# Embedding lookup plus positions: stores of two sequences, 16 KB for each partition, in place of one, 8 KB

## The chip, the cores and the metric

One core of one Trainium2 chip. The metric is the device time of one execution in microseconds (us), as the profiler gives it; the span of the profile is the same execution without about 1.7 us of launch.

A few words used below. GpSimd (POOL) issues the gathers: one gather is an indirect DMA that fetches 128 rows of the table, 2 KB each, 262 KB together. VectorE (DVE) adds, ScalarE (ACT) copies, SyncE (SP) issues loads and stores. The profile counts the packets of all DMA queues against the same 16 DMA engines. A "row" of a chunk is one 128 x 512 float32 piece, the product of one gather.

## The reference

```python
batch, seq_len, vocab_size, d_model = 32, 512, 50000, 512
def reference(indices, embedding_table, position_embed):
    token_embed = embedding_table[indices]
    return (token_embed + position_embed).astype(np.float32)
```

33.6 MB are gathered from random rows and 33.6 MB are written. Positions are 1 MB, indices 0.13 MB.

## The kernel before

A chunk is one sequence: partition p holds positions 4p to 4p+3, so K = 4 gathers fill it, and a whole store has 8 KB contiguous for each partition. The positions are copied once to PSUM, and VectorE adds them in place. The first and last sequences are stored in smaller pieces.

```python
P = 128; K = 4; SLOTS = 24; LANES = 16
HALVES = (2, 2); QUARTERS = (1, 1, 1, 1)
...
for b in range(B):
    if b <= 1 or b == B - 1:        parts = QUARTERS
    elif b <= 5 or b == B - 2:      parts = HALVES
    else:                           parts = (K,)
...
for g in range(B * K):                           # GpSimd
    b, k = divmod(g, K)
    ...
    ins = nc.gpsimd.indirect_dma_start(out=slots[b % SLOTS][:, k, :], ...)
    if g >= LANES:                               # at most 16 gathers outstanding
        ins._wait_ge(s_gather[g % LANES], rounds(g - LANES))
...
for b, at, n in stores:                          # SyncE
    nc.sync.dma_start(out=out_rows[b][:, at : at + n, :],
                      in_=slots[b % SLOTS][:, at : at + n, :]
    )._wait_ge(s_add, b * K + at + n).then_inc(done, 16)
```

## Time and profile before

| | before |
|---|---|
| time | 180.8 us (180.56 to 181.17, 3 runs) |
| last DMA packet, from the span's start | 174.5 us |
| GpSimd: last gather issued | 162.9 us |
| rate from 80 to 160 us | 415 GB/s |

From the page of the profile: the span, the DMA's busy share in 40 slices of 4.56 us (9 is 90% or more) with the GB/s moved under it, the two DMA queues (packets, MB, share of 16 engines; q0 carries the gathers, q1 loads and stores), the chain that ended last by engine, and the two large groups of instructions (busy us, mean ns of one, idle before).

```profile
span 182.4 us, 398 instructions
...
DMA  4999999999999999999999999999999999999910
GB/s 116 323 270 345 356 382 405 413 405 418 394 371 396 408 403 406 403 417 420 417 413 412 418 412 408 417 418 417 414 412 422 404 415 416 418 407 417 406 70 0
...
q0 software_dynamic: 10240, 33.56, 48.4%
q1 hardware_dynamic: 7392, 34.74, 46.6%
...
POOL 63%; issue 24%; DMA 6%; DVE 1%; SPq 0%; POOLq 0%
...
L121 POOL DMA_INDIRECT slot<-in_embedding_table_dram,idx_t x124 | 117.3, 946 | 37.8 <-issue 37.8
L150 DVE TENSOR_TENSOR slot<-slot,pos_ps 128x512 f32<-128x512 f32 x128 | 86.4, 687 | 80.0 <-issue 39.3
```

The list of waits (us in total, times, longest):

```profile
POOL slot L121 <- issue: 38.7, 127, 0.3
DVE slot L150 <- DMA slot<-in_embedding_table_dram,idx_t: 37.7, 38, 2.5
```

And the start, from the timeline (start us, duration, engine, instructions merged in one line):

```profile
8.49 2.70 DVE L150 TENSOR_TENSOR slot<-slot,pos_ps 128x512 f32<-128x512 f32 x4 [2.54 <-ACT pos_ps L156]
9.20 2.48 SPq L163 DMA_DIRECT2D out_dram<-slot  x4
```

How to read this. The chain names GpSimd, because GpSimd never rests: 128 gathers at 0.95 us and 0.30 us between them, never more (longest wait 0.3). It supplies 2 x 262 KB for each 1.25 us, 419 GB/s of work, counting the store that follows each gather. But the DMA row is full, and the DMA engines still work for 11.6 us after the last gather has been issued. So the DMA is the limit, with GpSimd close behind. The first add is at 8.5 us, the first store at 9.2 us.

### The profile page before, as it was taken

What the parts mean: (1) busy time and instruction counts of PE and PEld (TensorE: products, weight loads), DVE (VectorE), ACT (ScalarE), POOL (GpSimd) and SP (SyncE); (2) the same over time, 40 slices, a digit from 0 to 9 for tenths busy, and PEclk for the clock granted to TensorE, in tenths of its full rate; (3) what the DMA queues carried; (4) which work ended last, traced back from release to release, by engine and by line L of the source; (5) the groups of instructions that cost most, each with busy time, mean ns of one, the idle gap of its engine ahead of it and who ended that gap; (6) DMA issues with size and microseconds to landing.
All of it is one profiled execution on the core that took longest, in us unless ns stands there. A gap on an engine that the chain in (4) does not pass through costs nothing.

```text
span 182.4 us, 398 instructions
## 1 busy us (share of the span) xinstructions
PE 0.7 (0%) x4; PEld 0.6 (0%) x4; DVE 87.1 (48%) x130; ACT 3.6 (2%) x5; POOL 121.8 (67%) x134
## 2 busy tenths in 40 slices
PE   0100000000000000000000000000000000000000
PEld 0100000000000000000000000000000000000000
DVE  0253635546545445738355644455474655454400
ACT  2500000000000000000000000000000000000000
POOL 3777777777777777777777777777777777750000
DMA  4999999999999999999999999999999999999910
GB/s 116 323 270 345 356 382 405 413 405 418 394 371 396 408 403 406 403 417 420 417 413 412 418 412 408 417 418 417 414 412 422 404 415 416 418 407 417 406 70 0
DMA packets 17634, 68.32 MB, mean 375 GB/s; under 512 B 3008, under 2 KB 3008, under 8 KB 14560
## 3 DMA queue, kind: packets, MB, share of 16 engines
q0 software_dynamic: 10240, 33.56, 48.4%
q1 hardware_dynamic: 7392, 34.74, 46.6%
q14 instruction: 2, 0.02, 0.0%
HBM read 34.74 MB, written 33.55 MB: 374 GB/s over the span
## 4 chain that ended last, share of the span: by engine, by line
POOL 63%; issue 24%; DMA 6%; DVE 1%; SPq 0%; POOLq 0%
POOL slot L121 63%; DMA slot<-in_embedding_table_dram,idx_t 5%; DVE slot L150 1%; DMA idx<-in_indices_dram 1%; POOLq L119 0%; SPq L193 0%; SPq L94 0%
## 5 line engine op out<-in xcount | busy, mean ns | idle before, releaser
L121 POOL DMA_INDIRECT slot<-in_embedding_table_dram,idx_t x124 | 117.3, 946 | 37.8 <-issue 37.8
L150 DVE TENSOR_TENSOR slot<-slot,pos_ps 128x512 f32<-128x512 f32 x128 | 86.4, 687 | 80.0 <-issue 39.3
L121 POOL DMA_INDIRECT slot<-in_embedding_table_dram,idx x4 | 4.0, 993 | 2.5 <-DMA idx<-in_indices_dram 1.6
L139 DVE CAST idx_f<-idx_raw 32x512 f32<-32x512 int32 x1 | 0.4, 415 | 4.5 <-DMA idx_raw<-in_indices_dram 4.5
L156 ACT COPY pos_ps<-pos_sb 128x512 f32<-128x512 f32 x4 | 2.3, 587 | 4.4 <-DMA pos_sb<-in_position_embed_dram 4.4
L156 ACT ACT_TABLE_LOAD x1 | 1.3, 1283 | 1.0 <-SPq L94 1.0
L133 PE MATMUL turned<-ident,idx_f 32*128 32x32 f32 x4 | 0.7, 307 | 4.9 <-DVE idx_f L139 4.9
L142 DVE CAST idx_t<-turned 128x128 int32<-128x128 f32 x1 | 0.3, 291 | 0.8 <-PE turned L133 0.8
L133 PEld LDWEIGHTS turned<-ident,idx_f 32*128 32x128 f32 x4 | 0.6, 208 | 4.9 <-DVE idx_f L139 4.9
L106 POOL MEMSET ones<- 32x32 f32 x1 | 0.1, 115 | 0.5 <-SPq L94 0.5
L182 POOL MEMSET const-float32-0.0<- 128x1 f32 x1 | 0.1, 103 | 0.3 <-issue 0.3
L107 POOL TENSOR_SCALAR_AFFINE_SELECT ident<-ones 32x32 f32<-32x32 f32 x1 | 0.2, 203 | 0.1
L182 POOL MEMSET const-uint8-127<- 128x1 uint8 x1 | 0.1, 120 | 0.0
L182 POOL MEMSET const-bfloat16-1.0<- 128x1 bf16 x1 | 0.1, 114 | 0.0
L182 POOL MEMSET const-float32-1.0<- 128x1 f32 x1 | 0.1, 106 | 0.0
## 6 DMA issues: line engine op xcount, KB each, us to landing
out_dram<-slot SPq DMA_DIRECT2D x24, 1024.0 KB
out_dram<-slot SPq DMA_DIRECT2D x10, 512.0 KB
out_dram<-slot SPq DMA_DIRECT2D x12, 256.0 KB
slot<-in_embedding_table_dram,idx_t POOLq DMA_INDIRECT x124
pos_sb<-in_position_embed_dram SPq DMA_DIRECT2D x4, 256.0 KB, 3.0
idx_raw<-in_indices_dram SPq DMA_DIRECT2D x1, 128.0 KB, 3.0
slot<-in_embedding_table_dram,idx POOLq DMA_INDIRECT x4
idx<-in_indices_dram SPq DMA_DIRECT2D x1, 4.0 KB, 1.7
```

The source lines that it names most:

```text
L106: nc.gpsimd.memset(ones[:], 1.0).then_inc(s_ident, 1)
L107: nc.gpsimd.affine_select(out=ident[:], in_=ones[:], pattern=[[-1, B]], compare_op=mybir.AluOpType.is_equal, fill=0.0, base=0, channel_mul ...
L121: ins = nc.gpsimd.indirect_dma_start(out=slots[b % SLOTS][:, k, :], out_offset=None, in_=table, in_offset=bass.IndirectOffsetOnAxis(ap=whe ...
L133: ins = nc.tensor.transpose(turned[:, k, :], idx_f[:, :, k], ident[:])
L139: nc.vector.tensor_copy(out=idx_f[:].rearrange("b p k -> b (p k)"), in_=idx_raw[:, :, 0])._wait_ge(s_raw, 16).then_inc(s_cast, 1)
L142: nc.vector.tensor_copy(out=idx_t[:], in_=turned[:])._wait_ge(s_turn, K).then_inc(s_idx, 1)
L150: nc.vector.tensor_tensor(out=part, in0=part, in1=pos_ps[k][:], op=add)._wait_ge(s_gather[g % LANES], rounds(g)).then_inc(s_add, 1)
L156: nc.scalar.copy(out=pos_ps[k][:], in_=pos_sb[k][:])._wait_ge(s_pos[k], 16).then_inc(s_ps, 1)
L182: nc = _bacc.Bacc("TRN2", target_bir_lowering=False, num_devices=1)
```

## The change

Its intent: fewer and larger store packets. A chunk becomes two sequences; partition p holds eight positions of sequence p // 64, so a store has 16 KB contiguous for each partition. A position row is now needed in both halves of the partitions, so ScalarE copies each to both. Positions fill all of PSUM, and the index transpose borrows the last bank. Positions load as four DMAs of 64 partitions, two from ScalarE, ahead of the indices. The GpSimd drain at the end of the critical section is dropped.

```diff
-K = 4
-SLOTS = 24
+K = 8
+H = P // 2
+SLOTS = 11
...
-    out_rows = out.rearrange("b (p k) d -> b p k d", k=K)
+    out_rows = out.rearrange("(u s) (q k) d -> u (s q) k d", s=2, k=K)
...
-    for b in range(B):
-        if b <= 1 or b == B - 1:
-            parts = QUARTERS
-        elif b <= 5 or b == B - 2:
-            parts = HALVES
-        else:
-            parts = (K,)
+    for u in range(U):
+        parts = {0: (2, 2, 4), 1: (4, 4), U - 1: (4, 2, 1, 1)}.get(u, (K,))
...
-    with tc.tile_critical():
+    def load_pos(engine, k):
+        half, at = divmod(k, K // 2)
+        engine.dma_start(
+            out=pos_sb[half * H : (half + 1) * H, at : at + 2, :],
+            in_=pos_rows[:, k : k + 2, :],
+        ).then_inc(s_pos[k // 2], 16)
+
+    with tc.tile_critical(no_gpsimd_drain=True):
         nc.sync.dma_start(out=idx0[:], in_=idx_first).then_inc(s_first, 16)
+        load_pos(nc.sync, 0)
+        load_pos(nc.scalar, 4)
+        load_pos(nc.sync, 2)
+        load_pos(nc.scalar, 6)
         nc.sync.dma_start(out=idx_raw[:], ...).then_inc(s_raw, 16)
-        for k in range(K):
-            nc.sync.dma_start(out=pos_sb[k][:], in_=pos_rows[:, k, :])...
...
         for k in range(K):
-            nc.scalar.copy(out=pos_ps[k][:], in_=pos_sb[k][:])...
...
+            for to in range(2):
+                nc.scalar.copy(
+                    out=pos_ps[to * H : (to + 1) * H, k, :],
+                    in_=pos_sb[half * H : (half + 1) * H, at, :],
+                ).then_inc(s_ps, 1)
```

More of the change, by code (lines that the diff above doesn't have):

```diff
@@ L8 @@
 P = 128
-K = 4
-SLOTS = 24
+K = 8
+H = P // 2
+SLOTS = 11
 LANES = 16
-HALVES = (2, 2)
-QUARTERS = (1, 1, 1, 1)
 @with_exitstack
@@ L35 @@
     V, D = embedding_table.shape
-    assert S == P * K and B == 32
+    assert 2 * S == P * K and B % 2 == 0
     assert V < (1 << 24), "an index passes through float32"
-    idx_words = indices.bitcast(i32)
+    U = B // 2
+    idx_words = indices.bitcast(i32).rearrange("(u s) w -> u (s w)", s=2)
     idx_first = idx_words[0].rearrange("(p w) -> p w", p=P)
-    out_rows = out.rearrange("b (p k) d -> b p k d", k=K)
-    pos_rows = position_embed.rearrange("(p k) d -> p k d", k=K)
+    out_rows = out.rearrange("(u s) (q k) d -> u (s q) k d", s=2, k=K)
+    pos_rows = position_embed.rearrange("(q k) d -> q k d", k=K)
     table = embedding_table[:, :]
@@ L55 @@
     idx0 = sbuf("idx0", [P, 2 * K], i32)
-    idx_raw = sbuf("idx_raw", [B, S, 2], i32)
-    ones = sbuf("ones", [B, B], f32)
-    ident = sbuf("ident", [B, B], f32)
-    idx_f = sbuf("idx_f", [B, P, K], f32)
-    idx_t = sbuf("idx_t", [P, K, B], i32)
-    pos_sb = [sbuf(f"pos_sb{k}", [P, D], f32) for k in range(K)]
+    idx_raw = sbuf("idx_raw", [U, P * K, 2], i32)
+    ones = sbuf("ones", [U, U], f32)
+    ident = sbuf("ident", [U, U], f32)
+    idx_f = sbuf("idx_f", [U, P, K], f32)
+    idx_t = sbuf("idx_t", [P, K, U], i32)
+    pos_sb = sbuf("pos_sb", [P, K // 2, D], f32)
     slots = [sbuf(f"slot{n}", [P, K, D], f32) for n in range(SLOTS)]
-    turned = psum("turned", [P, K, B], f32)
-    pos_ps = [psum(f"pos_ps{k}", [P, D], f32) for k in range(K)]
+    pos_ps = psum("pos_ps", [P, K, D], f32)
+    turned = pos_ps[:, K - 1, : K * U].rearrange("p (k u) -> p k u", k=K)
     stores = []
-    for b in range(B):
-        if b <= 1 or b == B - 1:
-            parts = QUARTERS
-        elif b <= 5 or b == B - 2:
-            parts = HALVES
-        else:
-            parts = (K,)
+    for u in range(U):
+        parts = {0: (2, 2, 4), 1: (4, 4), U - 1: (4, 2, 1, 1)}.get(u, (K,))
         at = 0
         for n in parts:
-            stores.append((b, at, n))
+            stores.append((u, at, n))
             at += n
@@ L81 @@
     s_first, s_raw = sem("s_first"), sem("s_raw")
-    s_pos = [sem(f"s_pos{k}") for k in range(K)]
+    s_pos = [sem(f"s_pos{n}") for n in range(4)]
     s_gather = [sem(f"s_gather{n}") for n in range(LANES)]
-    s_out = {b: sem(f"s_out{b}") for b in range(B - SLOTS)}
+    s_out = {u: sem(f"s_out{u}") for u in range(U - SLOTS)}
     s_rest = sem("s_rest")
@@ L92, in rounds @@
         return 16 * (g // LANES + 1)
-    with tc.tile_critical():
+    def load_pos(engine, k):
[5 more added lines that the diff above has]
+    with tc.tile_critical(no_gpsimd_drain=True):
         nc.sync.dma_start(out=idx0[:], in_=idx_first).then_inc(s_first, 16)
+        load_pos(nc.sync, 0)
+        load_pos(nc.scalar, 4)
+        load_pos(nc.sync, 2)
+        load_pos(nc.scalar, 6)
         nc.sync.dma_start(
-            out=idx_raw[:], in_=idx_words.rearrange("b (s w) -> b s w", w=2)
+            out=idx_raw[:], in_=idx_words.rearrange("u (s w) -> u s w", w=2)
         ).then_inc(s_raw, 16)
-        for k in range(K):
-            nc.sync.dma_start(out=pos_sb[k][:], in_=pos_rows[:, k, :]).then_inc(
-                s_pos[k], 16
-            )
         nc.gpsimd.memset(ones[:], 1.0).then_inc(s_ident, 1)
         nc.gpsimd.affine_select(
-            out=ident[:], in_=ones[:], pattern=[[-1, B]],
+            out=ident[:], in_=ones[:], pattern=[[-1, U]],
             compare_op=mybir.AluOpType.is_equal, fill=0.0, base=0,
@@ L112 @@
         nc.gpsimd.wait_ge(s_first, 16)
-        for g in range(B * K):
-            b, k = divmod(g, K)
+        for g in range(U * K):
+            u, k = divmod(g, K)
             if g == K:
                 nc.gpsimd.wait_ge(s_idx, 1)
-            if b >= SLOTS and k == 0:
-                done = sum(1 for x in stores if x[0] == b - SLOTS)
-                nc.gpsimd.wait_ge(s_out[b - SLOTS], 16 * done)
-            where = idx0[:, 2 * k : 2 * k + 1] if b == 0 else idx_t[:, k, b : b + 1]
+            if u >= SLOTS and k == 0:
+                done = sum(1 for x in stores if x[0] == u - SLOTS)
+                nc.gpsimd.wait_ge(s_out[u - SLOTS], 16 * done)
+            where = idx0[:, 2 * k : 2 * k + 1] if u == 0 else idx_t[:, k, u : u + 1]
             ins = nc.gpsimd.indirect_dma_start(
-                out=slots[b % SLOTS][:, k, :],
+                out=slots[u % SLOTS][:, k, :],
                 out_offset=None,
@@ L139 @@
         nc.vector.tensor_copy(
-            out=idx_f[:].rearrange("b p k -> b (p k)"), in_=idx_raw[:, :, 0]
+            out=idx_f[:].rearrange("u p k -> u (p k)"), in_=idx_raw[:, :, 0]
         )._wait_ge(s_raw, 16).then_inc(s_cast, 1)
-        nc.vector.tensor_copy(out=idx_t[:], in_=turned[:])._wait_ge(
+        nc.vector.tensor_copy(out=idx_t[:], in_=turned)._wait_ge(
             s_turn, K
         ).then_inc(s_idx, 1)
-        for g in range(B * K):
-            b, k = divmod(g, K)
-            if b == 0:
-                nc.vector.wait_ge(s_ps, k + 1)
-            part = slots[b % SLOTS][:, k, :]
+        for g in range(U * K):
+            u, k = divmod(g, K)
+            if u == 0:
+                nc.vector.wait_ge(s_ps, 2 * (k + 1))
+            part = slots[u % SLOTS][:, k, :]
             nc.vector.tensor_tensor(
-                out=part, in0=part, in1=pos_ps[k][:], op=add
+                out=part, in0=part, in1=pos_ps[:, k, :], op=add
             )._wait_ge(s_gather[g % LANES], rounds(g)).then_inc(s_add, 1)
         for k in range(K):
-            nc.scalar.copy(out=pos_ps[k][:], in_=pos_sb[k][:])._wait_ge(
-                s_pos[k], 16
-            ).then_inc(s_ps, 1)
+            half, at = divmod(k, K // 2)
+            if k % 2 == 0:
+                nc.scalar.wait_ge(s_pos[k // 2], 16)
+            if k == K - 1:
+                nc.scalar.wait_ge(s_idx, 1)
+            for to in range(2):
[3 more added lines that the diff above has]
+                ).then_inc(s_ps, 1)
         rest = 0
-        for b, at, n in stores:
-            done = s_out.get(b, s_rest)
+        for u, at, n in stores:
+            done = s_out.get(u, s_rest)
             rest += done is s_rest
             nc.sync.dma_start(
-                out=out_rows[b][:, at : at + n, :],
-                in_=slots[b % SLOTS][:, at : at + n, :],
-            )._wait_ge(s_add, b * K + at + n).then_inc(done, 16)
+                out=out_rows[u][:, at : at + n, :],
+                in_=slots[u % SLOTS][:, at : at + n, :],
+            )._wait_ge(s_add, u * K + at + n).then_inc(done, 16)
         nc.sync.wait_ge(s_rest, 16 * rest)
```

## The prediction

> **What bounds the kernel now.** The DMA engines. The page's slices show a DMA share of 9 tenths from the second slice to the thirty-eighth, and 404 to 422 GB/s in most slices after the seventh; the last packet ends at 174.5 us. GpSimd is a close second: its gathers are strictly periodic (0.95 us busy + 0.30 us issue, never a longer wait in the list of waits), so 128 take 160 us, from 2.98 to 162.9 us. That is 2 x 262 KB per 1.25 us = 419 GB/s of supply against about 415 moved. The chain of waits names GpSimd (63% + 24% issue), but after its last gather the DMA works 11.6 us more: 4.8 MB of backlog. VectorE (87 us) binds nothing. After the last packet the span goes on 7.9 us with no recorded work: closing drains and barriers.
>
> **What the change does.**
> 1. Store packets. The packet records give medians of 84, 159 and 309 ns for 2, 4 and 8 KB: about 9 ns fixed and 37 ns per KB; my estimate for 16 KB is 0.61 us. Data packets on the hardware queue fall from 6432 to about 3090; 3300 x 9 ns / 16 engines = 1.9 us; in the steady state about 419 instead of 415 GB/s. All of it is on the critical path, because the DMA is.
> 2. Ramp. Stores of 2, 2, 4, 4, 4 and then 8 rows replace stores of 1 and 2 rows; the first add waits for the index transpose (now behind the position loads): about 9.5 us instead of 8.5. ScalarE has 16 copies at 0.59 us instead of 4, but its 1.2 us for each k keeps up with the gathers. A store of 8 rows must wait for 10 us of gathers, so the engines may idle 0 to 2 us before the backlog has built. This is bounded: they can idle only while little is outstanding, that is, while ahead.
> 3. Arbitration. The Trainium skill ("DMA: Bandwidth & Descriptors", Queues, rings and completion order) says that an engine round-robins between queues by packet. The trace agrees: 36 packets of 8 KB beside 30 gather packets of 4 KB in one microsecond. With 16 KB a store gets four fifths of the bandwidth while it runs; gathers bunch between stores, 11 to 13 outstanding at the peak, below the 16 lanes. GpSimd should wait rarely, and at no cost.
> 4. Slots: 11 of two sequences (22 instead of 24): far from binding.
> 5. End. The GpSimd drain at the close of the critical section goes; later drains stay. Estimate, not measurable in this trace: 1 us of the 7.9.
>
> **Sum.** 180.8 - 1.9 (packets) - 1.0 (drain) + 0.5 (ramp) = 178.4 us; 8 in 10 for 176.2 to 180.6. Faster by over 2% (below 177.2): 0.27; within 2%: 0.68; slower: 0.05.
>
> **What would show it.** Packets: a 16 KB store packet near 0.61 us, slices at 415 to 425 GB/s in the steady state. Ramp: first VectorE add near 9.5 us, gaps in the DMA row between 20 and 40 us. Arbitration: adds in bursts, GpSimd still at 1.25 us. Drain: last packet to end of span near 6.9 us. Last packet near 173 us.
>
> **What would make it wrong.** The slow first 16 us (264 to 314 GB/s between 5 and 15 us, gather packets up to 460 ns) may come from the 2 KB stores; then their removal gains 2 us more. The drain may cost 0 or 3 us. Gathers starved behind 16 KB packets may hit the lanes and leave the engines idle afterwards, or the last gathers may land late and lay the last adds and stores bare.

## The result

| | before | after |
|---|---|---|
| time, same rounds | 180.68 us (180.25 to 181.17, 4 runs) | 183.13 us (182.72 to 183.71, 4 runs) |
| ratio, 95% interval | | 1.0137 (1.0098 to 1.0176) |
| last DMA packet | 174.4 us (control below) | 176.8 us |
| last packet to end of span ("closing part" below) | 4.2 us (control below) | 4.2 us |

Slower by 1.4%, where 1.3% faster was forecast; by the 2% rule the class is "same". The prediction gave "within 2%" the highest chance (0.68), but it expected the time on the other side of before, so that this class came true is luck.

The same lines of the changed kernel's page (slices of 4.53 us):

```profile
span 181.0 us, 395 instructions
...
DMA  5999999999999999999999999999999999999990
GB/s 134 190 341 268 397 388 392 406 362 411 336 407 368 419 424 384 436 391 422 408 414 430 373 435 393 432 397 424 406 412 427 378 446 382 423 407 414 420 397 3
...
q0 software_dynamic: 10240, 33.56, 49.9%
q1 hardware_dynamic: 3504, 34.22, 46.2%
q10 hardware_dynamic: 160, 0.52, 1.1%
...
POOL 65%; issue 23%; DMA 6%; DVE 0%; SPq 0%
...
L128 POOL DMA_INDIRECT slot<-in_embedding_table_dram,idx_t x120 | 113.4, 945 | 36.6 <-issue 36.6
L157 DVE TENSOR_TENSOR slot<-slot,pos_ps 128x512 f32<-128x512 f32 x128 | 85.5, 687 | 75.3 <-DMA slot<-in_embedding_table_dram,idx_t 74.2
```

Its list of waits:

```profile
DVE slot L157 <- DMA slot<-in_embedding_table_dram,idx_t: 74.2, 35, 5.7
POOL slot L128 <- issue: 38.7, 127, 0.3
```

Its start, and the first store of a whole chunk, from the timeline:

```profile
11.56 1.87 DVE L157 TENSOR_TENSOR slot<-slot,pos_ps 128x512 f32<-128x512 f32 x3
...
12.86 0.37 SPq L179 DMA_DIRECT2D out_dram<-slot  x1
```

```profile
38.77 0.33 SPq L179 DMA_DIRECT2D out_dram<-slot  x1
...
47.30 0.69 DVE L157 TENSOR_TENSOR slot<-slot,pos_ps 128x512 f32<-128x512 f32 x1 [5.66 <-DMA slot<-in_embedding_table_dram,idx_t]
```

What is to be seen. Packets fell from 17634 to 13906 on the page, 7392 to 3664 (3504 + 160) on the hardware queues, as planned. GpSimd is as before: 945 ns, longest wait 0.3 us. But the GB/s row now swings (362, 411, 336, 407, 368) where before's stands near 410, and it is at 190 in the second slice, where before's has 323. VectorE waits for gathers up to 5.7 us at a time, where before had 2.5. Only the length of the single wait has grown: in all VectorE idles 75.3 us against 80.0 (before's list books a part of it under "issue"). The add at 47.30 us comes only when the chunk's store, issued at 38.77 us, has gone through: the last of its 16 KB packets ends at 46.9 us. The first add is at 11.6 us, not 8.5.

One trap: the spans of the two recorded profiles (182.4 and 181.0 us) say that the change is faster. The profile of before came from an execution of 184.1 us, 3.4 us above its own timed runs. The control below shows why they can't be subtracted.

### Where the microseconds are, from the packet records

Each DMA packet's duration is in the trace. I split the sum of durations over 16 engines into a base (each packet at the median for its size: 9 ns for a semaphore write, 84, 159, 309 and 611 ns for 2, 4, 8 and 16 KB), an excess (what packets took beyond that), and the rest up to the last packet (idle engines, less some overlap of packets). before_again is the control of before.

```
us for each engine     base    excess   rest    sum = last packet
before_again          166.4      6.8     1.2       174.4
after                 164.5     11.6     0.7       176.8
difference             -1.9     +4.8    -0.4        +2.4
```

The saving of 1.9 us is there to a tenth. It is more than eaten by packets that took longer than their size asks. Of the 4.8 us of excess, 2.8 arise before 20 us (against 1.0 less idle time there), 1.6 between 30 and 60 us and 0.9 after 60; from 20 to 30 us it is 0.5 less than before.

This is one profile of each. The other profiles with the change's stores throughout (after_drain, after_again and after_idx_first below) have the same base, an excess of 11.6 to 12.1 and a rest of 1.6 to 2.0 us; before in its recorded profile has an excess of 7.2 and a rest of 0.9. So the excess is the large part in every draw, and up to about 1 us of the loss can be idle engines.

### The profile page after: what moved, and what is told of

It is laid out like the page before. It is cut to its first block, busy times and chain, and to the rows that moved or that the text cites. A ratio compares the mean times of both kernels' runs of the same rounds, so it can differ in the third digit from the quotient of the medians.

```text
span 181.0 us, 395 instructions
## 1 busy us (share of the span) xinstructions
PE 1.1 (1%) x8; PEld 1.0 (1%) x8; DVE 86.4 (48%) x130; ACT 10.6 (6%) x17; POOL 121.7 (67%) x134
## 2 busy tenths in 40 slices
DMA packets 13906, 68.32 MB, mean 377 GB/s; under 512 B 2624, under 2 KB 2624, under 8 KB 11712
## 3 DMA queue, kind: packets, MB, share of 16 engines
q1 hardware_dynamic: 3504, 34.22, 46.2%
## 4 chain that ended last, share of the span: by engine, by line
POOL 65%; issue 23%; DMA 6%; DVE 0%; SPq 0%
POOL slot L128 65%; DMA slot<-in_embedding_table_dram,idx_t 5%; DMA idx<-in_indices_dram 1%; DVE slot L157 0%; SPq L209 0%; SPq L100 0%
## 5 line engine op out<-in xcount | busy, mean ns | idle before, releaser
L128 POOL DMA_INDIRECT slot<-in_embedding_table_dram,idx_t x120 | 113.4, 945 | 36.6 <-issue 36.6
L157 DVE TENSOR_TENSOR slot<-slot,pos_ps 128x512 f32<-128x512 f32 x128 | 85.5, 687 | 75.3 <-DMA slot<-in_embedding_table_dram,idx_t 74.2
L128 POOL DMA_INDIRECT slot<-in_embedding_table_dram,idx x8 | 7.8, 970 | 3.7 <-issue 2.1
L169 ACT COPY pos_ps<-pos_sb 64x512 f32<-64x512 f32 x16 | 9.3, 583 | 2.8 <-DMA pos_sb<-in_position_embed_dram 2.5
L146 DVE CAST idx_f<-idx_raw 16x1024 f32<-16x1024 int32 x1 | 0.7, 680 | 9.5 <-DMA idx_raw<-in_indices_dram 9.5
L140 PE MATMUL pos_ps<-ident,idx_f 16*128 16x16 f32 x8 | 1.1, 268 | 10.3 <-DVE idx_f L146 10.3
L140 PEld LDWEIGHTS pos_ps<-ident,idx_f 16*128 16x128 f32 x8 | 1.0, 197 | 10.3 <-DVE idx_f L146 10.3
```

Source lines behind the costliest of these rows:

```text
L128: ins = nc.gpsimd.indirect_dma_start(out=slots[u % SLOTS][:, k, :], out_offset=None, in_=table, in_offset=bass.IndirectOffsetOnAxis(ap=whe ...
L140: ins = nc.tensor.transpose(turned[:, k, :], idx_f[:, :, k], ident[:])
L146: nc.vector.tensor_copy(out=idx_f[:].rearrange("u p k -> u (p k)"), in_=idx_raw[:, :, 0])._wait_ge(s_raw, 16).then_inc(s_cast, 1)
L157: nc.vector.tensor_tensor(out=part, in0=part, in1=pos_ps[:, k, :], op=add)._wait_ge(s_gather[g % LANES], rounds(g)).then_inc(s_add, 1)
L169: nc.scalar.copy(out=pos_ps[to * H : (to + 1) * H, k, :], in_=pos_sb[half * H : (half + 1) * H, at, :],).then_inc(s_ps, 1)
```

## The experiments

Runs of one call share the chip and the runs of before. The theories:

- R (ramp): the coarse first stores (2, 2, 4, 4, 4, 8 rows) leave the engines without work early.
- B (burst): whole chunks of eight rows give long bursts of stores with gathers bunched between them.
- W: the 16 KB packet itself, which would take four fifths of an engine's time if its packets alternated with 4 KB gather packets.
- P and L: the half-partition position loads; the late indices and late first add.
- D: the drain matters.

### First call: control, drain, and stores of four rows

before_again is the kernel before, unchanged.

> The kernel before once more, unchanged, as a control, because the profiled execution of before (184.1 us, span 182.4) is 3.4 us above its own timed runs (180.7) while that of the change (182.7) is one of its timed runs. If the recorded profile was a slow draw in its last part (7.9 us from the last packet to the end): ratio 1.00, span near 179.0, last packet near 174.5 and a closing part near 4 to 5 us. If the closing part is really 7.9 us and the extra is an effect of profiling: the span is 182.4 again.

Measured: 180.58 us, ratio 1.0009 (0.9983 to 1.0036), span 178.6, last packet at 174.4, closing part 4.2 us. So the recorded profile of before has the same DMA work (174.5 us) and only a longer end.

```diff
-    with tc.tile_critical():
+    with tc.tile_critical(no_gpsimd_drain=True):
```

> The kernel before with the GpSimd drain at the close of the critical section taken away and nothing else. Theory D (the drain costs 1 us or more of the closing part, up to the 3.7 us by which the closing parts of the two profiles differ): ratio 0.98 to 0.995, last packet to end shorter by that much. Rival (the later drains take over what it waited for, the profile of before was a slow draw): ratio 0.998 to 1.002.

Measured: 180.68 us, ratio 1.0009 (0.9978 to 1.0039). The drain is worth nothing. after_drain is the reverse edit in the changed kernel:

> The changed kernel with the drain put back. Theory D: 1 to 3.7 us longer than the change, so a ratio to before of 1.02 to 1.034. Rival: the same as the change, 1.012 to 1.016.

Measured: 183.56 us, ratio 1.0172 (1.0144 to 1.0201), against 1.0137 (1.0098 to 1.0176) for the change; the intervals overlap. Theory D falls. The instruction records tell why:

```
start us  ns     instruction of GpSimd, line
before_again
174.95   2515   DRAIN, line 94  (end of the critical section)
177.54     34   DRAIN, line 193 (end of the program)
after
177.51     13   NOP,   line 100 (the drain's place)
177.59   2515   DRAIN, line 209 (end of the program)
```

The first drain that GpSimd meets after its gathers takes 2515 ns in either place, and SyncE's closing steps wait for GpSimd behind it. Dropping one only hands the cost to the next.

after_store4 stores each later chunk in two halves:

```diff
-        parts = {0: (2, 2, 4), 1: (4, 4), U - 1: (4, 2, 1, 1)}.get(u, (K,))
+        parts = {0: (2, 2, 4), 1: (4, 4), U - 1: (4, 2, 1, 1)}.get(u, (K // 2, K // 2))
```

> The changed kernel with two stores of four rows (8 KB packets) for each chunk in place of one of eight (16 KB packets); start, mapping and drain as in the change. Theory B (bursts of whole chunks cost the time: the stretch from 35 to 50 us, where the change falls back by 0.56 MB, and gather packets of 172 ns in the stretches without stores): 1 to 2 us shorter than the change, ratio near 1.003. Rival S (the later start: first add at 11.6 instead of 8.5 us, 0.54 MB behind at 20 us): within 0.5 us of the change, ratio 1.010 to 1.016.

Measured: 181.45 us, ratio 1.0044 (1.0015 to 1.0073). The whole-chunk store costs 1.7 us (183.13 - 181.45; the ratios, 1.0137 and 1.0044 to before, say the same). The base of the change is 0.8 us smaller than that of after_store4, so what the burst loses elsewhere is 2.5 us. These two parts come from different calls, and the intervals of the two ratios leave about 0.9 us of room; against after_drain of the same call after_store4 is 2.1 us shorter. The stages show where. The profiled execution of after_store4 is the slowest of its six (182.19 us, last packet at 176.3), so its profile shows less than the whole gain. Busy time of each engine, clock, DMA share and GB/s in three stretches, first the control of before, then the change, then after_store4:

```profile
core 0: us, PE busy (x) PEld busy (x) DVE busy (x) ACT busy (x) POOL busy (x), PEclk, DMA share, GB/s
...
40.00:50.00 10.00, 0.00 (x0) 0.00 (x0) 5.90 (x9) 0.00 (x0) 7.56 (x9) 1.00 1.03 411
50.00:60.00 10.00, 0.00 (x0) 0.00 (x0) 5.18 (x8) 0.00 (x0) 7.56 (x9) 1.00 1.01 402
80.00:160.00 80.00, 0.00 (x0) 0.00 (x0) 43.32 (x65) 0.00 (x0) 60.50 (x65) 1.00 1.02 414
```

```profile
40.00:50.00 10.00, 0.00 (x0) 0.00 (x0) 3.89 (x7) 0.00 (x0) 7.56 (x9) 1.00 0.98 368
50.00:60.00 10.00, 0.00 (x0) 0.00 (x0) 4.91 (x8) 0.00 (x0) 7.57 (x9) 1.00 1.02 393
80.00:160.00 80.00, 0.00 (x0) 0.00 (x0) 43.49 (x65) 0.00 (x0) 60.51 (x65) 1.00 1.02 412
```

```profile
40.00:50.00 10.00, 0.00 (x0) 0.00 (x0) 4.97 (x8) 0.00 (x0) 7.56 (x9) 1.00 1.01 387
50.00:60.00 10.00, 0.00 (x0) 0.00 (x0) 5.42 (x8) 0.00 (x0) 7.56 (x9) 1.00 1.02 404
80.00:160.00 80.00, 0.00 (x0) 0.00 (x0) 43.25 (x64) 0.00 (x0) 60.50 (x65) 1.00 1.02 414
```

From 40 to 50 us the change moves 368 GB/s where before moves 411, with the DMA share at 0.98 against 1.03; VectorE gets 7 adds where before had 9. After_store4 is between at 387, and from 80 to 160 us it is level with before (414) while the change is at 412. (The view counts a packet where it starts. By where packets end, the change's rate from 80 to 160 us is 410 GB/s, against 414 for before and 414 for after_store4.)

### Second call: the loads, the burst alone, the order

The first call ran on chip 9; from here on the calls fell on chips 10, 15, 10 and 2, where before takes 184.1 to 184.4 us, as in its recorded profile. The last packet is where it was (174.5 to 175.0 us); the closing part is 7.6 to 8.2 us for the kernels that end there, but only 5.5 to 6.8 for those whose last packet comes at 175.8 to 178.4 us. In the instruction records SyncE's own closing steps, 7 to 28 ns in the control, take up to 1.4 us there:

```
SyncE, closing of before (long)     before_again (short)
EVENT_SEMAPHORE  1397 ns            28 ns
EVENT_SEMAPHORE   713               28
NOP               691               13
DRAIN             699                7
```

Why is not shown. What matters: on such a chip SyncE is late anyhow, and up to about 2 us of a later last packet are hidden. So for these calls I compare the last packet too; each is one draw; before and its variants without a burst lay between 174.4 and 175.0 in six profiles.

before_pos128 and before_pos64 are the kernel before with its positions in one tile and 4 KB pieces:

```diff
-        for k in range(K):
-            nc.sync.dma_start(out=pos_sb[k][:], in_=pos_rows[:, k, :])...
+        for k in range(0, K, 2):                                      # before_pos128
+            nc.sync.dma_start(out=pos_sb[:, k : k + 2, :], in_=pos_rows[:, k : k + 2, :])...
+        for k in range(0, K, 2):                                      # before_pos64
+            for half, engine in enumerate((nc.sync, nc.scalar)):
+                at = slice(64 * half, 64 * half + 64)
+                engine.dma_start(out=pos_sb[at, k : k + 2, :], in_=pos_rows[at, k : k + 2, :])...
```

> The kernel before with its four position loads of 128 partitions x 2 KB made two of 128 partitions x 4 KB, as a control for the next run. All theories: 256 packets fewer, 0.1 to 0.2 us; ratio 0.997 to 1.001. Packets of the load near 160 to 200 ns.

> The same bytes in the same 4 KB pieces, but as four loads of 64 partitions, two from SyncE and two from ScalarE, as the change loads them; indices first as before. Theory P (the two half-partition loads in flight together are slow by themselves: packets of 240 to 280 ns in the change where 159 is the norm): 0.7 to 1.2 us longer than before_pos128, load packets over 220 ns, 1.5 us or more of excess packet time between 3 and 10 us. Rival O (only the order matters: indices behind the positions): within 0.3 us of before_pos128, load packets under 200 ns.

Measured: 184.42 and 184.41 us, ratio 1.0004 for both (0.9992 to 1.0016 and 0.9991 to 1.0017). The half loads are slow by themselves: medians of 292 and 249 ns a packet on the two queues against 159 in before_pos128, and 1.75 against 0.50 us of excess for loads and stores from 3 to 10 us. The Trainium skill ("SBUF — State Buffer", "Can I just issue two DMAs to hit both halves?") says that two such DMAs nearly serialize. The packet records fit: each packet took 1.6 to 1.8 times as long. No run times one half load alone, so that they serialize is not shown here. But nothing comes of it: at 20 us 5.48 MB have landed with the half loads and 5.40 with the whole ones, and the last packet is at 174.6 and 175.0. The engines had idle time there to absorb it (2.2 us of it were left before 20 us, against 3.4 in before_pos128). Theory P was right about the packets and wrong about the time.

before_burst8 has before's 8 KB packets, but holds stores back so that two sequences go out back to back:

```diff
+        def due(b, upto):
+            if 6 <= b < B - 2 and b % 2 == 0:
+                return (b + 2) * K          # the first waits for the second's adds
+            return b * K + upto
...
-            )._wait_ge(s_add, b * K + at + n).then_inc(done, 16)
+            )._wait_ge(s_add, due(b, at + n)).then_inc(done, 16)
```

> The kernel before with the stores of 8 KB packets held back so that two whole sequences are stored back to back (from sequence 6 on, except the last two): the burst of the change without its 16 KB packets. Theory B (the burst: gathers run alone for longer, at about 172 instead of 159 ns a packet): 1.0 to 2.0 us longer, ratio 1.005 to 1.011, gather excess in 80 to 160 us near 0.6 us for each 20 us instead of 0.3. Rival W (the 16 KB packet itself: a store with four fifths of the bandwidth, packets of over 1 us between 44 and 57 us): ratio 0.998 to 1.003 and no such excess.

Measured: 185.11 us, ratio 1.0036 (1.0020 to 1.0053), last packet at 177.2: 2.2 us later than before_pos128 of the same call, with exactly the packets of before (base 166.4 us). So the burst costs without any 16 KB packet. The ratio lies below what B expected (1.005 to 1.011), which the long closing part explains at least in part. The excess of the gathers from 80 to 160 us was 0.44 us for each 20 us, between B's 0.6 and before's 0.3: whether the 16 KB packet adds its share in the change is taken up below.

after_idx_first puts the index load back ahead of the positions in the changed kernel (one statement of three lines moved).

> The changed kernel with the index load put back in front of the position loads. Rival O: the first add near 9 to 9.5 us instead of 11.6, 0.7 to 1.0 us shorter than the change (near 182.3 us), with 0.3 MB more moved at 20 us. Theory P: the first add comes earlier, but waits for positions, and the time is within 0.4 us of the change.

Measured: the first add at 9.7 us instead of 11.6, but 185.70 us, ratio 1.0068 (1.0052 to 1.0084), last packet at 178.3, and 5.02 MB at 20 us. The change itself ended at 176.8 in its first profile and at 178.4 in the third call, where its ratio was 1.0051. Nothing was gained; theory L falls, as far as one draw can tell.

### Third call: the start

after_again is the change unchanged. after_fine gives it before's store sizes for the first 24 rows; after_fine4 does that, puts the index load first, and stores later chunks in halves:

```diff
-        parts = {0: (2, 2, 4), 1: (4, 4), U - 1: (4, 2, 1, 1)}.get(u, (K,))
+        parts = {0: (1,) * 8, 1: (2,) * 4, 2: (2,) * 4, U - 1: (4, 2, 1, 1)}.get(u, (K,))             # after_fine
+        parts = {0: (1,) * 8, 1: (2,) * 4, 2: (2,) * 4, U - 1: (4, 2, 1, 1)}.get(u, (K // 2, K // 2)) # after_fine4
```

> The changed kernel once more, unchanged, as the control of this call: the last call ran on a chip where before took 184.4 us and closed 7.7 to 8.0 us after its last packet, so kernels are compared within a call and by the time of the last packet. Expected: ratio 1.010 to 1.017 on a chip like the first; last packet near 177.

> The changed kernel with the store sizes of before over the first 24 rows (8 of one row, 8 of two), later chunks whole as in the change. Theory R (coarse first stores leave the DMA without work at the start): bytes moved at 20 us 5.2 to 5.5 MB instead of 4.9, last packet 0.5 to 1 us earlier than after_again. But the step to 8 rows then only comes later, so a part may return as a gap near 50 us. Rival L (the late first add, 11.6 instead of 8.5 us, sets the start): 4.9 to 5.1 MB at 20 us and the same time.

> The change with all three undone at once: index load first, store sizes of before over the first 24 rows, two stores of four rows for each later chunk. If coarse stores and the start are the whole loss: ratio to before 0.993 to 1.001, last packet 174 to 175 us. If something else of the change costs (rows of a 16 KB pitch, two-half loads, PSUM in one tile): ratio above 1.003.

> The run before_burst8 once more (the kernel before, stores of 8 KB packets two sequences at a time), for its time on a chip without the long closing part. Theory B: last packet 2 to 2.6 us later than before's 174.5 again, and on a chip like the first the time 1.5 to 2.5 us longer, ratio 1.008 to 1.014. Rival: ratio below 1.004 again and the late last packet was a single draw.

Measured: after_again 185.15 us, ratio 1.0051 (1.0038 to 1.0064), last packet 178.4; the last packet is 1.4 us later than expected, and the ratio is below what was expected because this chip closes late. after_fine 184.97 us, the same ratio 1.0051, last packet 176.6, and 5.31 MB at 20 us instead of 4.73: the start is regained with the first add as late as ever, as R says, but this chip's closing shows none of it in the time. after_fine4 184.09 us, ratio 0.9999 (0.9986 to 1.0012), last packet 175.8, 0.8 us later than the latest that was expected. burst8_again 184.25 us, ratio 1.0016 (1.0003 to 1.0029), last packet 177.1. The late last packet is no single draw; the time says little on this chip.

### Fourth and fifth calls: second draws, and a version without the burst

before_fewer is before_pos128 with five fewer stores (first sequence 1, 1, 2 rows, second 2, 2, last 2, 1, 1, last but one whole; the "8" in its expectation is a miscount); the others repeat earlier kernels (burst8_3 and burst8_4: before_burst8; fine_2: after_fine; fine4_2 and fine4_3: after_fine4).

> Burst of two sequences with 8 KB packets, third draw. Theory B: last packet at 176.5 to 177.5 us; on a chip that closes in 4.2 us the time is 1.5 to 2.5 us above before, ratio 1.008 to 1.014; on one with the long closing part 1.001 to 1.005. Rival: last packet before 175.5.

> after_fine, second draw: start of before, later chunks whole. Theory R and B together: 20 us: 5.2 to 5.5 MB; last packet 176 to 177 (start regained, burst still paid); on a chip that closes in 4.2 us ratio 1.005 to 1.011.

> after_fine4, second draw: start of before, index first, stores of four rows. If start and burst are the whole loss: last packet 174 to 175.8, ratio 0.994 to 1.002. If above 1.003 on a chip that closes in 4.2 us, something else of the change costs as well.

> The kernel before with position loads of 4 KB pieces (two instead of four) and 8 fewer small stores: first sequence 1, 1, 2 rows, second 2, 2, last 2, 1, 1, last but one whole. Packet arithmetic alone saves 0.5 us: ratio 0.996 to 0.999, last packet 0.3 to 0.7 us earlier than before. If the coarser first stores cost what the change's did, it gives that back: ratio 0.999 to 1.003.

> The kernel before with stores of two sequences back to back. Theory B: where the closing part is 4.2 us, ratio 1.008 to 1.014 and last packet 176.5 to 177.2; where it is long, ratio 1.001 to 1.005 with the same last packet. Rival: below these.

> The change with start, index order and stores of four rows given back. If start and burst are the whole loss: where the closing part is 4.2 us, ratio 0.996 to 1.003 and last packet 174.3 to 175.8. If another part of the change costs: above 1.004.

Measured, all with the long closing part:

| run | time, us | ratio (95%) | last packet | MB at 20 us | MB at 60 us | MB at 160 us |
|---|---|---|---|---|---|---|
| burst8_3 | 184.82 | 1.0030 (1.0012 to 1.0048) | 176.6 | 5.51 | 20.82 | 61.67 |
| burst8_4 | 185.07 | 1.0046 (1.0033 to 1.0059) | 177.8 | 5.47 | 20.68 | 61.47 |
| fine_2 | 185.08 | 1.0042 (1.0025 to 1.0059) | 176.7 | 5.24 | 20.57 | 61.49 |
| fine4_2 | 184.63 | 1.0019 (1.0003 to 1.0035) | 174.7 | 5.42 | 21.22 | 62.50 |
| fine4_3 | 184.36 | 0.9997 (0.9980 to 1.0015) | 175.0 | 5.34 | 21.15 | 62.46 |
| before_fewer | 184.29 | 1.0000 (0.9984 to 1.0016) | 174.5 | 5.42 | 21.30 | 62.55 |
| for comparison: before_again (first call) | 180.58 | 1.0009 | 174.4 | 5.49 | 21.35 | 62.56 |
| after | 183.13 | 1.0137 | 176.8 | 4.93 | 20.39 | 61.43 |

The two corners, in the same stretches as above, burst8_4 (before with the burst added) and fine4_3 (the change with burst and coarse start taken away):

```profile
40.00:50.00 10.00, 0.00 (x0) 0.00 (x0) 6.37 (x11) 0.00 (x0) 7.56 (x9) 1.00 0.97 370
50.00:60.00 10.00, 0.00 (x0) 0.00 (x0) 3.93 (x6) 0.00 (x0) 7.56 (x9) 1.00 1.00 372
80.00:160.00 80.00, 0.00 (x0) 0.00 (x0) 43.49 (x65) 0.00 (x0) 60.50 (x65) 1.00 1.02 411
```

```profile
40.00:50.00 10.00, 0.00 (x0) 0.00 (x0) 5.43 (x9) 0.00 (x0) 7.56 (x9) 1.00 1.02 404
50.00:60.00 10.00, 0.00 (x0) 0.00 (x0) 4.82 (x7) 0.00 (x0) 7.56 (x9) 1.00 0.99 381
80.00:160.00 80.00, 0.00 (x0) 0.00 (x0) 42.34 (x63) 0.00 (x0) 60.49 (x65) 1.00 1.02 414
```

The burst alone takes the stretch from 40 to 60 us down to 370 and 372 GB/s and the long stretch to 411; the change without burst and coarse start has 404 and 381 there, and 414. Before had 408, 384 and 415 in its recorded profile and 411, 402 and 414 in the control.

By last packets the change ended at 176.8 and 178.4, after_fine at 176.6 and 176.7, after_fine4 at 175.8, 174.7 and 175.0 (means 177.6, 176.7 and 175.2): about 1.0 us for the coarse first stores and 1.5 for the whole-chunk stores. The three profiles of before in which nothing but the drain differs ended at 174.4 to 174.9 (mean 174.6), so that 0.6 us may remain to the change's other edits; that lies within the scatter of the draws.

No version beat before. before_fewer has 0.6 us less base than before. It had moved less at 30 us (8.93 MB against 9.24 in before_again), but had all but caught up at 60, and its last packet came 0.4 us before that of before_pos128, from which it differs in its stores alone and whose base is 0.4 us larger. So whether a slightly coarser start gives its saving back is not shown: one profile, and a chip that hides up to 2 us, cannot settle tenths.

### What the burst does, from the packet records

Three things can be read.

1. At the step to eight rows there is a gap. Before a first burst may start, eight gathers must have landed, and the engines have only gathers, which GpSimd supplies at half the engines' rate (262 KB in 1.25 us, 210 GB/s, against 415). In burst8_4, from 48.5 to 49 us, 9.8 of 16 engines held a gather packet and none a store packet, and in the change the gather packets of 38.75 to 39.25 us took 233 to 285 ns, with 12.7 to 12.9 engines busy.
2. In the first bursts stores run almost alone (0 to 5 of 16 engines held a gather packet from 40.25 to 46 us in the change), and towards their end the store packets slow down: from 40 to 70 us, 31 of the change's 378 packets of 16 KB took over 1.5 times the median of 611 ns (up to 1296), and 62 of burst8_4's 512 packets of 8 KB (up to 705, median 309), but 4 of 592 in before_again. What holds them is not shown.
3. Later, in the change, gathers run in company less often. From 80 to 160 us a gather packet takes 161 to 163 ns beside stores and 166 to 171 ns when no store is in flight, in every kernel. In before_again 32% of them are alone and the mean is 164 ns (in before's recorded profile 45%, with the same mean); in the change 74% and 168 ns. A store costs 153.5 ns for each 4 KB instead of 155.6. So for each 4 KB gathered and stored, 2 ns are saved on the store and 4 lost on the gather. Why gathers alone are slower is not shown.

The third point goes with the 16 KB stores more than with the burst. In the four burst8 profiles 45 to 47% of these gathers are alone, against 32 to 45% in before's kernels without a burst, and the gathers' excess from 80 to 160 us is 1.5 to 1.8 us, against 1.1 to 1.4 in those kernels and 2.1 to 2.3 in every kernel with 16 KB stores; with stores of four rows it is 1.3 to 1.5. So the burst alone, whose last packets came at 176.6 to 177.8 us (before's at 174.4 to 175.0), costs mostly by the first two points, and theory W stays open for a part of the change's loss; the difference of the excesses, about 0.6 us, is my estimate of its size. No run has 16 KB packets without the burst.

## Why the prediction was wrong

Predicted 178.4 us, in a range of 176.2 to 180.6; measured 183.13. The last packet was expected near 173 us and came at 176.8. Two terms of the sum failed, the ramp and the drain, and a third is missing: stores of whole chunks were priced by their packets alone and cost more than they saved.

1. What bounds the kernel: right. The DMA is the limit. GpSimd kept its 1.25 us in all kernels and never waited longer than 0.3 us.
2. Store packets, -1.9 us: right as arithmetic. The 16 KB packet has a median of 611 ns (0.61 predicted) and the base fell by 1.9 us. What failed is the next step, "in the steady state about 419 instead of 415 GB/s. All of it is on the critical path": from 80 to 160 us the change ran at 410, not 419. I priced each packet by its size and took the price as independent of what else is in flight. The trace of before had the warning in it: gather packets with a median of 159 ns and a mean of 170.
3. Ramp, +0.5 us: mechanism right, size wrong. If packets gave -1.9 and the drain 0, the remaining terms must be +4.4 us to end at +2.5 (183.13 - 180.68 = 2.45). The runs split it, with up to 0.9 us of room: 2.5 us for whole-chunk stores, the missing term (after_store4 is 1.7 us shorter with a base 0.8 us larger), and 1.8 us for the start, which is the ramp's true size (after_store4 is still 0.8 us above before, 1.0044 of 180.46, although its base is 1.0 us smaller). That the remainder of after_store4 is the start is inferred: the finer start was run alone only on a chip that closes late, where the bytes at 20 us and the last packet show it and the time does not. The first add at 11.6 instead of 9.5 us was a miss as well, but after_idx_first shows that it does not matter. The "gaps in the DMA row between 20 and 40 us" did not show there (its digits are all 9): the packet records have a partial one near 39 us, and it is the GB/s row that swings, on to 60 us.
4. Why "bounded: they can idle only while ahead" failed: the argument is about idle engines, and in the first profile the engines were hardly idle (rest 0.7 against 1.2 us; up to 2.0 in other draws). Mostly they were busy with packets that took longer. An engine that holds a packet counts as busy however slowly the bytes move: from 40 to 50 us the DMA share is 0.98 at 368 GB/s.
5. Arbitration: adds in bursts and GpSimd at 1.25 us, right; "at no cost", wrong, and this is where the missing term belongs. The Trainium skill's round robin by packet ("DMA: Bandwidth & Descriptors", Queues, rings and completion order) shows in the later bursts, 19, 21 and 25 store packets beside 19, 19 and 11 gather packets in the three microseconds from 158 us on, but in the first ones less so, 25, 21 and 15 beside 18, 3 and 9 from 43 us on; whether too few gathers were ready there is not shown. Gathers did bunch; what I didn't see is that a gather without a store beside it is slower.
6. Drain, -1.0 us: wrong, it was worth 0. The drain takes 2.5 us, but at whichever drain comes first, and the later ones stayed.
7. Slots: right; 11 slots never held anything up.
8. "What would make it wrong" listed the last adds laid bare and GpSimd hitting its lanes. Neither came. It did not list the burst; the nearest it came is "gathers starved behind 16 KB packets", with another consequence.

## What to carry to other kernels

Before making a transfer larger, count what it takes from the mix: fewer packets were worth 1.9 us here, while a coarser start, longer waits for a whole chunk, bursts of stores, and gathers running alone cost 4.4 together. On an engine shared by two streams, read a packet's duration alone and in company from the trace, not its median by size. Raise the grain of stores in small steps, and expect the step itself to cost; and don't count on a dropped drain if another follows on the same path.

## What the Trainium skill lacked or had wrong

- "DMA: Bandwidth & Descriptors" (Rules for kernel authors) advises 128 partitions and at least 1 MiB for each DMA. It does not say what a still larger store costs a second stream that shares the engines. Here stores of 2 MB in place of 1 MB ended 1.7 us later (183.13 against 181.45 us), with a smaller sum of packet medians.
- The same page (Queues, rings and completion order) describes the round robin. It does not say that a packet's duration depends on its company: gather packets of 4 KB took 161 to 163 ns beside stores and 166 to 171 ns without.
- The same page (SWDGE vs HWDGE vs iDMA) gives a packet, for the software path, as preferably at most 4096 bytes. The hardware queue's store packets were 8192 and 16384 bytes, at medians of 309 and 611 ns. Whether what the page and what the profile call a packet are the same is not shown.
- "SBUF — State Buffer" ("Can I just issue two DMAs to hit both halves?") warns of two half-partition DMAs, and their packets were slow here (249 and 292 ns against 159). It lacks that this can cost nothing, where the engines have idle time (5.48 against 5.40 MB at 20 us).
- No page that I read has the cost of GpSimd's drain after gathers: 2515 ns for the first drain, 34 ns for the one that followed it in before_again.
- No page that I read has the two closings: 4.2 us, or 5.5 to 8.2 us with SyncE's steps at up to 1.4 us each. 14 of these 18 runs had the second kind, which hid up to about 2 us of differences.
